# How a head's queries, keys and values are fetched in an attention core: one broadcast transfer on GpSimd's queue, or two of 64 rows on SyncE's

## The chip, the cores and the metric

The kernel runs on one core of a Trainium2 chip. Its time is the device time of one execution in microseconds; a kernel's figure is the median of its runs. The engines of a core work through their own instruction streams and wait for each other by semaphores: TensorE (PE) multiplies, VectorE (DVE), ScalarE (ACT) and GpSimd (POOL) work on tiles, SyncE (SP) issues transfers. Transfers are carried out by 16 DMA engines, whichever engine issues them.

## The reference

A trunk of two layers on 1024 tokens of 1024 features: a retention layer and a chunked attention layer, each behind an RMSNorm and followed by an MLP with squared ReLU, and a last norm. The change is in the attention:

```python
def _chunk_attention(h, w_in, rel_bias, w_out):
    q, k, v = jnp.split(h @ w_in, 3, axis=-1)          # 16 heads of 64 features
    ...
    def one_chunk(c):                                  # 64 queries, the 576 keys up to their chunk's end
        s = jnp.einsum('bqhd,bkhd->bhqk', qb, kb) * scale + bias[None]
        s = jnp.where(valid, s, -jnp.inf)
        p = jax.nn.softmax(s, axis=-1)
        return jnp.einsum('bhqk,bkhd->bqhd', p, vb)
    o = lax.map(one_chunk, jnp.arange(nc))
    return o @ w_out
```

## The kernel before, in words

Everything is float32. Each operand of a product is split into a high part, rounded to the tensor engine's float32r, and a low part, the rest; three products (lines 162 to 164, one each of high-high, low-high and high-low) carry a full one.

The attention has two stages. The **projection** computes queries and keys for pairs of heads (`qk_proj`) and then values. A result `t` is split into `dhi` and the remainder (lines 727 and 729), and SyncE stores both to scratch tensors in DRAM (line 733): `qA` for queries, `kA` for keys, `vA` for values (line 756). A stored key tensor of a head is `[64 features, 2 parts, 1024 tokens]`. Weights come in units of 512 KB (`wraw`, line 146, two buffers), also issued by SyncE, and are split by ACT (`whi`, line 137) and DVE or POOL (`wlo`, line 141).

The **core** goes over 16 heads with four units each; a unit `g` holds two blocks of 128 queries. Each head needs four things, loaded by `load_head`: `qh` (128 x 1024: high and low queries, 64 features each, stacked on the partitions), `kk` (128 x 2 x 1024: the high keys and the low keys, both on the upper and on the lower 64 partitions, so that two passes give all four partial products), the bias `bt`, and the values `vst`. `qh`, `kk` and `bt` have two buffers each, `vst` three: the keys of head h go where those of head h-2 were, and the transfer can start once TensorE has read those for the last time. In a unit, lines 846 and 847 compute scores into `pS`, line 851 (DVE) adds the bias and takes the extreme, line 855 (ACT) the exponentials, line 857 (POOL) scales them; line 875 (PE) transposes them to `pt`, ACT and DVE split the result, and line 887 (PE) multiplies by the values. One step of the output projection of earlier heads (`att_out`, the filler, lines 162 to 164 with `oh`, `ol`) is issued with each unit from the 19th unit on.

The order in which instructions stand on each engine is decided by a scheduler from the order of the code and its own estimate of the times; each engine then works through its list in that order. The queues of SP and POOL are lists of this kind: a transfer that waits for its buffer holds back all that stands behind it on that queue.

Heads 0 and 1 are fetched ahead, during the projection; the others within the core.

Of the kernel before, what the change touches and what calls it, by code (L numbers as in the profile page):

```python
# [9 lines left out]
F32 = mybir.dt.float32  # L10
# [3 lines left out]
PSUM = bass.MemoryType.PSUM  # L14
DRAM = bass.MemoryType.DRAM

P = 128
# [9 lines left out]
DH = 64  # L27
# [15 lines left out]
def _tables():  # L43
    """Position tables: they depend on the shapes alone."""
    import numpy as np

    half = DK // 2
    inv = np.exp(-np.float32(np.log(10000.0)) * np.arange(half, dtype=np.float32) / np.float32(half))
    ang = (np.arange(S, dtype=np.float32)[:, None] * inv.astype(np.float32)[None, :]).astype(np.float64)
    cos = np.cos(ang).T.astype(np.float32)  # L50
    sin = np.sin(ang).T.astype(np.float32)
    lg = _log_gamma()
    jp = np.arange(S) % HT
    vdec = np.exp(-lg[None, :] * (jp[:, None] + 1.0)) * RET_SCALE
    vdec = vdec.reshape(NB, P, RH).transpose(1, 0, 2)
    ip = np.arange(HT)
    odec = np.exp(lg[None, :] * (ip[:, None] + 1.0)).reshape(HT // P, P, RH).transpose(1, 0, 2)
    j = np.arange(P)[:, None]
    i = np.arange(P)[None, :]
    same = (j // CHUNK) == (i // CHUNK)  # L60
    mask = np.zeros((P, RH, P))
    for h in range(RH):
        m = np.where(i >= j, 1.0, 0.0)
        mask[:, h, :] = np.where(same & (i < j), np.exp(2.0 * lg[h] * (j - i)), m)
    f = lambda a: np.ascontiguousarray(a, dtype=np.float32)
    return {
        "cos": f(cos),
        "sin": f(sin),
        "vdec": f(vdec),
        "odec": f(odec),  # L70
        "odec2": f(odec * odec),
        "mask": f(mask),
    }
# [3 lines left out]
def trunk_kernel(ctx: ExitStack, tc: tile.TileContext, I, out):  # L77
# [34 lines left out]
    def load_gains(psp, pl, parts, g0):  # L112
        """Gains of 128 features in a row each, turned so that the features lie on the partitions."""
        n = sum(src.shape[0] for src in parts)
        rows = pl.tile([n, P], F32, name="grows", tag=f"grows{g0}")
        r = 0
        for src in parts:
            DMA.dma_start(out=rows[r:r + src.shape[0], :], in_=src)
            r += src.shape[0]

        def turn():
            pg = psp.tile([P, n], F32, name="pg", tag="ps")
            nc.tensor.transpose(pg, rows, ident[0:n, 0:n])
            nc.vector.tensor_copy(out=gall[:, g0:g0 + n], in_=pg)
        return turn
# [8 lines left out]
    def split(src, hi, lo, hi_eng="act", lo_eng="dve"):  # L134
        """hi: src rounded to the tensor engine's float32r; lo: what is left of src, exactly."""
        if hi_eng == "act":
            nc.scalar.copy(out=hi, in_=src)  # L137
        else:
            nc.vector.tensor_copy(out=hi, in_=src)
        eng = nc.vector if lo_eng == "dve" else nc.gpsimd  # L140
        eng.tensor_tensor(out=lo, in0=src, in1=hi.bitcast(F32), op=ALU.subtract)  # L141

    def wload(src, kb, cols):
        """Fetch one weight unit [128, kb, cols] (1024 columns)."""
        raw = wp.tile([P, kb, cols], F32, name="wraw", tag="wraw", bufs=2)
        DMA.dma_start(out=raw, in_=src.rearrange("(k p) c -> p k c", p=P))
        return raw
# [11 lines left out]
    def mm3(ps, lhs, rhs, start, stop):  # L159
        """Three products that carry a float32 product of split operands."""  # L160
        (lh, ll), (rh, rl) = lhs, rhs
        nc.tensor.matmul(ps, lhsT=lh, rhs=rh, start=start, stop=False)  # L162
        nc.tensor.matmul(ps, lhsT=lh, rhs=rl, start=False, stop=False)  # L163
        nc.tensor.matmul(ps, lhsT=ll, rhs=rh, start=False, stop=stop)  # L164
# [4 lines left out]
    def rsqrt_newton(sd, v, y):  # L169
        """y = v ** -0.5, one Newton step past the square root's table."""  # L170
        nc.scalar.activation(sd, v, AF.Sqrt)
        nc.vector.reciprocal(out=y, in_=sd)
        nc.vector.scalar_tensor_tensor(out=sd, in0=v, scalar=-0.5, in1=y, op0=ALU.mult, op1=ALU.mult)
        nc.vector.tensor_tensor(out=sd, in0=sd, in1=y, op=ALU.mult)
        nc.vector.scalar_tensor_tensor(out=y, in0=sd, scalar=1.5, in1=y, op0=ALU.add, op1=ALU.mult)

# [1 line left out]
    class Norm:  # L178
# [28 lines left out]
        def finish(self, psp, hf, col=False, row=True):  # L207
            """r = rsqrt(mean + eps) of a half: along the free axis in rB, along the partitions in rcol."""
            ah = self.gp.tile([P, HT], F32R, name="ah", tag="ah")
# [18 lines left out]
    def up_group(psp, norm, w, hf):  # L228
        """128 output features of one half of the tokens."""
        hi, lo = w  # L230
        ps = psp.tile([P, HT], F32, name="ps", tag="ps")
        for kb in range(NB):
            mm3(ps, (hi[:, kb, :], lo[:, kb, :]), (norm.hi[kb][hf], norm.lo[kb][hf]), kb == 0, kb == NB - 1)
        return ps
# [5 lines left out]
    def proj_tok(psp, norm, src, evac):  # L240
        """512 output features, tokens on the partitions: one bank for each block of tokens."""
        pss = [psp.tile([P, HT], F32, name="ps", tag="ps") for _ in range(NB)]
# [10 lines left out]
    def down(box, src, nk, rhs, hi_eng="act", lo_eng="dve"):  # L253
        """h += W^T rhs for nk blocks of features, one group at a step. box holds the PSUM pool and, where
        the blocks are final, their norm; blocks that were final before the norm was there follow."""
        cols = 1024 // nk
# [35 lines left out]
    class Filler:  # L292
        """Steps of a product that are issued between other work."""

# [42 lines left out]

    # ================= retention =================
    vS = [dram.tile([S, DV], F32, name=f"vS{i}") for i in range(RH)]
# [137 lines left out]
    with ExitStack() as ph:  # L477
# [6 lines left out]
        with ExitStack() as st:  # L484
# [5 lines left out]

            # Loads run in the order of use, a ring of raw tiles ahead of the splits.
            items = [(hd, hf, what) for hd in range(RH) for hf in range(2) for what in ("q", "k", "v0", "v1")]
# [33 lines left out]
            def turn_k(hd):  # L526
                """Keys of the first half with the tokens on the partitions."""
                kt[hd] = th, tl = [cp.tile([P, 4, DK], F32R, name=n, tag=n, bufs=1) for n in ("kth", "ktl")]
# [45 lines left out]
            def outs(hd, hf, pr):  # L574
                """Retention of two blocks of queries and their normalised rows."""
                pss, mv = [], cp.tile([P, 2, 2], F32, name="mv", tag="mv", bufs=2)
# [115 lines left out]

    # ================= first MLP =================
    with ExitStack() as ph:
# [3 lines left out]

    # ================= chunked attention =================
    w_in = I["att_w_in"][0]  # L700
# [6 lines left out]
    with ExitStack() as ph:  # L707
# [57 lines left out]
        def load_q(hd):  # L765
            T[hd, "q"] = cq.tile([P, S], F32R, name="qh", tag="qh", bufs=2)
            nc.gpsimd.dma_start(out=T[hd, "q"], in_=qA[hd // 2][hd % 2].rearrange("z f c -> (z f) c"))

        def load_k(hd):
            t = cq.tile([P, 2, S], F32R, name="kk", tag="kk", bufs=2)  # L770
            src = kA[hd // 2][hd % 2]
            nc.gpsimd.dma_start(out=t.rearrange("p z s -> p (z s)"), in_=bass.AP(tensor=src.tensor, offset=src.offset, ap=[[0, 2], [2 * S, DH], [1, 2 * S]]))
            T[hd, "k"] = [t[:, 0, :], t[:, 1, :]]
# [18 lines left out]
    with ExitStack() as ph:  # L792
# [7 lines left out]
        with ExitStack() as st:  # L800
# [8 lines left out]
            def load_head(hd, step):  # L809
                """Stacks that give all four partial products of q k in two passes, values and bias."""  # L810
                if step == 0:
# [8 lines left out]
                else:  # L820
                    t = cp.tile([P, NB, P], F32R, name="vst", tag="vst", bufs=3)
                    nc.gpsimd.dma_start(out=t, in_=vA[hd // 8][:, (hd % 8) * P:(hd % 8 + 1) * P].rearrange("(t p) c -> p t c", p=P))
                    T[hd, "v"] = t
# [11 lines left out]
            def scores(hd, g, z):  # L835
                """Probabilities of one block of queries; scores and bias come negated."""
                Q = 2 * g + z
# [97 lines left out]

    # ================= second MLP and the last norm =================
    with ExitStack() as ph:
        psp = pool(ph, "psF", None, 8, PSUM)
        with ExitStack() as st:
# [4 lines left out]
            def last(src, rhs):  # L944
                """The last part of the product, half by half: one half leaves while the other is computed."""
                ws = []
# [63 lines left out]
```

## Time and profile before

| | |
|---|---|
| median of 3 runs | 3041.18 us (3039.38 to 3042.13) |
| span of the profiled execution, first to last instruction | 3039.2 us |
| TensorE busy | 2871.2 us, 94% of the span |
| VectorE, ScalarE, GpSimd busy | 1319.7, 880.3, 432.5 us |
| mean granted clock of TensorE | 0.971 of full speed |
| core stage | about 1900 to 2290 us of the span |
| projection stage | about 1630 to 1900 us |

The span is that of the profiled execution; the time of that execution is not told beside it, and the runs shown lie 0.2 to 2.9 us above the span. A stage in which TensorE is not busy is where time can be won; what ends its idle stretches there is what bounds it.

### The profile page before, as it was taken

The page shows a single profiled execution, that of the slowest core. Times are in us where ns is not written, and L with a number is a line of the kernel's source. Part 1 is how long each engine was busy: PE and PEld are TensorE (multiplying, and loading weights), DVE is VectorE, ACT ScalarE, POOL GpSimd, SP SyncE. Part 2 cuts the span into 40 slices and gives each one's busy share as a digit, 9 for nine tenths or more (in the row PEclk, how much of TensorE's full clock was granted, in tenths as well). Part 3 has the DMA queues.
Part 4 walks back from the last instruction along what each step waited for, and adds up shares of the span by engine and source line. Part 5 has one row for each costly group of instructions (what it writes and reads, how often), then busy time and mean ns, then how long its engine had stood idle before and what let it go on. Part 6 is the DMA issues. An engine that isn't in the chain of part 4 may idle for free.

```text
span 3039.2 us, 33109 instructions
## 1 busy us (share of the span) xinstructions
PE 2871.2 (94%) x13178; PEld 2376.4 (78%) x13178; DVE 1319.7 (43%) x2194; ACT 880.3 (29%) x1484; POOL 432.5 (14%) x439
## 2 busy tenths in 40 slices
PE   8999999899999999999999899576879999999998
PEld 7888888677778888888888788465767888888887
DVE  6331133555565333333346233465668333333335
ACT  4012222432342221112223122564655111222213
POOL 4320000322230000000002000454533000000002
PEclk9999999899999999999999999788989999999999
DMA  4323333432111111111114546645521111111111
GB/s 138 106 87 103 108 105 96 158 104 90 63 49 43 48 49 49 49 49 49 49 46 133 149 147 162 120 95 115 113 68 42 49 49 49 49 46 45 49 49 70
DMA packets 258122, 245.86 MB, mean 81 GB/s; under 512 B 25048, under 2 KB 209440, under 8 KB 255920
## 3 DMA queue, kind: packets, MB, share of 16 engines
q1 hardware_dynamic: 220896, 207.19, 22.4%
q0 software_dynamic: 35584, 33.61, 5.1%
q10 hardware_dynamic: 1488, 2.95, 0.3%
q8 instruction: 103, 1.69, 0.2%
q14 instruction: 51, 0.42, 0.0%
HBM read 189.09 MB, written 57.19 MB: 81 GB/s over the span
## 4 chain that ended last, share of the span: by engine, by line
PE 83%; DMA 10%; DVE 4%; POOL 1%; ACT 1%; issue 1%; SPq 0%; POOLq 0%; ACTq 0%; DVEq 0%
PE ps L162 26%; PE ps L163 26%; PE ps L164 26%; DMA kk<-kA 7%; PE po L887 1%; PE pt L875 1%; DVE hlo L190 0%; DMA kA<-dhi 0%; PE pS L846 0%; POOL acc L200 0%; DMA xt<-in_x_dram 0%; PE pS L847 0%; PE pt L629 0%; DMA wraw<-in_att_w_in_dram 0%; DMA qA<-dhi 0%
## 5 line engine op out<-in xcount | busy, mean ns | idle before, releaser
L162 PE MATMUL ps<-hhi,whi 128*128 128x512 f32 x1792 | 699.3, 390 | 12.5 <-ACT whi L137 9.3
L163 PE MATMUL ps<-hlo,whi 128*128 128x512 f32 x1792 | 698.8, 390 | 1.4 <-DVE hlo L190 1.4
L164 PE MATMUL ps<-hhi,wlo 128*128 128x512 f32 x1792 | 698.5, 390 | 1.0 <-DVE wlo L141 0.9
L137 ACT CAST whi<-wraw 128x1024 fp32r<-128x1024 f32 x220 | 231.6, 1053 | 1255.1 <-PE ps L163 1023.4
L280 DVE TENSOR_TENSOR h<-ps,h 128x512 f32<-128x512 f32 x368 | 253.6, 689 | 467.5 <-PE ps L164 465.4
L162 PEld LDWEIGHTS ps<-hhi,whi 128*128 128x128 f32 x1792 | 337.2, 188 | 83.6 <-ACT whi L137 10.0
L163 PEld LDWEIGHTS ps<-hlo,whi 128*128 128x128 f32 x1792 | 337.3, 188 | 72.1 <-DVE hlo L190 2.1
L164 PEld LDWEIGHTS ps<-hhi,wlo 128*128 128x128 f32 x1792 | 337.1, 188 | 72.2 <-DVE wlo L141 2.1
L162 PE MATMUL ps<-uh,whi 128*128 128x512 f32 x960 | 379.7, 396 | 0.0
L163 PE MATMUL ps<-ul,whi 128*128 128x512 f32 x960 | 379.7, 396 | 0.0
L164 PE MATMUL ps<-uh,wlo 128*128 128x512 f32 x960 | 379.7, 396 | 0.0
L141 DVE TENSOR_TENSOR wlo<-wraw,whi 128x1024 fp32r<-128x1024 f32 x213 | 266.7, 1252 | 239.4 <-ACT whi L137 239.3
L200 POOL TENSOR_TENSOR acc<-acc,sq 128x512 f32<-128x512 f32 x70 | 102.4, 1465 | 1418.0 <-ACT sq L199 1412.2
L324 DVE SCALAR_TENSOR_TENSOR t<-ps,rB 128x512 f32<-128x512 f32 x128 | 88.0, 691 | 320.6 <-PE ps L164 320.6
L162 PEld LDWEIGHTS ps<-uh,whi 128*128 128x128 f32 x960 | 180.3, 188 | 43.7
L164 PEld LDWEIGHTS ps<-uh,wlo 128*128 128x128 f32 x960 | 180.3, 188 | 43.6
L163 PEld LDWEIGHTS ps<-ul,whi 128*128 128x128 f32 x960 | 180.3, 188 | 43.6
L846 PE MATMUL pS<-kk,qh 128*128 128x320 f32 (+1 forms) x192 | 70.0, 370 | 107.2 <-DMA kk<-kA 102.4
L325 ACT ACTIVATE t<-t 128x512 f32<-128x512 f32 x128 | 80.5, 630 | 262.1 <-DVE t L324 262.1
L162 PE MATMUL ps<-whi,hhi 128*128 128x512 f32 x384 | 149.4, 389 | 0.3 <-DVE vt L755 0.3
L164 PE MATMUL ps<-whi,hlo 128*128 128x512 f32 x384 | 149.4, 389 | 0.0
L163 PE MATMUL ps<-wlo,hhi 128*128 128x512 f32 x384 | 149.4, 389 | 0.0
(188 smaller groups left out, 3760.3 us busy)
## 6 DMA issues: line engine op xcount, KB each, us to landing
wraw<-in_mlp_w_dram SPq DMA_DIRECT2D x128, 512.0 KB, 3.7
wraw<-in_ret_w_in_dram SPq DMA_DIRECT2D x48, 512.0 KB, 4.0
kk<-kA POOLq DMA_DIRECT2D x16, 1024.0 KB, 27.4
wraw<-in_att_w_in_dram SPq DMA_DIRECT2D x24, 512.0 KB, 3.9
vS<-t SPq DMA_DIRECT2D x32, 256.0 KB, 2.0
gS<-t SPq DMA_DIRECT2D x32, 256.0 KB, 2.1
wraw<-in_ret_w_out_dram SPq DMA_DIRECT2D x16, 512.0 KB, 3.5
raw<-vS SPq DMA_DIRECT2D x16, 512.0 KB, 4.5
```

The costliest lines, as they stand in the source:

```text
L137: nc.scalar.copy(out=hi, in_=src)
L141: eng.tensor_tensor(out=lo, in0=src, in1=hi.bitcast(F32), op=ALU.subtract)
L162: nc.tensor.matmul(ps, lhsT=lh, rhs=rh, start=start, stop=False)
L163: nc.tensor.matmul(ps, lhsT=lh, rhs=rl, start=False, stop=False)
L164: nc.tensor.matmul(ps, lhsT=ll, rhs=rh, start=False, stop=stop)
L200: nc.gpsimd.tensor_tensor(out=self.acc[hf], in0=self.acc[hf], in1=sq, op=ALU.add)
L280: nc.vector.tensor_tensor(out=hv, in0=ps, in1=hv, op=ALU.add)
L324: nc.vector.scalar_tensor_tensor(out=t, in0=res[hf], scalar=0.0, in1=rB[:, hf * HT:(hf + 1) * HT], op0=ALU.max, op1=ALU.mult)
L325: nc.scalar.activation(t, t, AF.Square)
L846: nc.tensor.matmul(ps[:, y, :hw], lhsT=qs, rhs=kh[:, ks], start=True, stop=False)
L875: nc.tensor.transpose(pt[:, c - done:c - done + P], pr[:, (kb - k0) * P:(kb - k0 + 1) * P], ident)
L887: nc.tensor.matmul(po[:, oc:oc + n], lhsT=T[hd, "v"][:, kb, :], rhs=t[:, off[kb]:off[kb] + n], start=i == 0, stop=i == len(seq) - 1)
```

## The change

The queries and the values of a head are issued by SyncE and no longer by GpSimd. The keys of a head came in one transfer of GpSimd, whose source names the 64 feature rows twice by an outer dimension of two with step 0; now they come in two transfers of SyncE, each of the 64 rows to one half of the partitions. Bytes, buffers and arithmetic are as they were.

```diff
         def load_q(hd):
             T[hd, "q"] = cq.tile([P, S], F32R, name="qh", tag="qh", bufs=2)
-            nc.gpsimd.dma_start(out=T[hd, "q"], in_=qA[hd // 2][hd % 2].rearrange("z f c -> (z f) c"))
+            DMA.dma_start(out=T[hd, "q"].bitcast(F32), in_=qA[hd // 2][hd % 2].rearrange("z f c -> (z f) c"))

         def load_k(hd):
             t = cq.tile([P, 2, S], F32R, name="kk", tag="kk", bufs=2)
             src = kA[hd // 2][hd % 2]
-            nc.gpsimd.dma_start(out=t.rearrange("p z s -> p (z s)"), in_=bass.AP(tensor=src.tensor, offset=src.offset, ap=[[0, 2], [2 * S, DH], [1, 2 * S]]))
+            for z in range(2):
+                DMA.dma_start(out=t[z * DH:(z + 1) * DH].bitcast(F32), in_=src)
             T[hd, "k"] = [t[:, 0, :], t[:, 1, :]]
...
                 else:
                     t = cp.tile([P, NB, P], F32R, name="vst", tag="vst", bufs=3)
-                    nc.gpsimd.dma_start(out=t, in_=vA[hd // 8][:, (hd % 8) * P:(hd % 8 + 1) * P].rearrange("(t p) c -> p t c", p=P))
+                    DMA.dma_start(out=t.bitcast(F32), in_=vA[hd // 8][:, (hd % 8) * P:(hd % 8 + 1) * P].rearrange("(t p) c -> p t c", p=P))
```

`DMA` is `nc.sync`, SyncE's queue. The changed kernel is one line longer, so lines behind 772 count one more there.

On SyncE's queue in the middle of the core there stood only the biases of heads 6 to 9 (`skew_10933` to `skew_10936`) and a unit of the output weights:

```order
L779 DMA bt<-skew_10933 64x576 x2
L779 DMA bt<-skew_10934 64x576 x2
L146 DMA wraw<-in_att_w_out_dram 128x2x512
L779 DMA bt<-skew_10935 64x576 x2
L779 DMA bt<-skew_10936 64x576 x2
```

Now the same place reads, from head 7 on (`kA_10921` holds heads 6 and 7, `kA_10922` heads 8 and 9):

```order
L767 DMA qh<-qA_10913 128x1024
L773 DMA kk<-kA_10921 64x2048 x2
L780 DMA bt<-skew_10934 64x576 x2
L146 DMA wraw<-in_att_w_out_dram 128x2x512
L823 DMA vst<-vA_10909 128x8x128
L767 DMA qh<-qA_10914 128x1024
L773 DMA kk<-kA_10922 64x2048 x2
L780 DMA bt<-skew_10935 64x576 x2
L823 DMA vst<-vA_10909 128x8x128
L767 DMA qh<-qA_10914 128x1024
L773 DMA kk<-kA_10922 64x2048 x2
```

The values, queries and keys of each head stand ahead of its bias, and the output weights stand ahead of the values of head 8. On GpSimd's queue the loads of head 8 stood between the scalings of probabilities (`pr`) of earlier units; these are the rows before:

```order
L141 TENSOR_TENSOR wlo<-wraw,whi 128x1024
L857 TENSOR_SCALAR pr<-pr,sm 128x384
L822 DMA vst<-vA_10909 128x8x128
L857 TENSOR_SCALAR pr<-pr,sm 128x512
L141 TENSOR_TENSOR ol<-osum,oh 64x256
L767 DMA qh<-qA_10914 128x1024
L857 TENSOR_SCALAR pr<-pr,sm 128x640
L772 DMA kk<-kA_10922 128x1x2048
L857 TENSOR_SCALAR pr<-pr,sm 128x640
```

In the changed kernel the same stretch of GpSimd's queue holds the arithmetic alone, in the same sequence. The third place is SyncE's queue in the projection, where the loads of head 1 (`qA_10910`, `kA_10918`) come in between the stores of the keys of heads 6 and 7 (`kA_10921`) and the value weights; this is a piece of the difference:

```order
-L733 DMA kA_10921<-dhi 64x512 x2
-L733 DMA kA_10921<-t 64x512 x2
-L146 DMA wraw<-in_att_w_in_dram 128x2x512 x4
+L733 DMA kA_10921<-dhi 64x512
+L733 DMA kA_10921<-t 64x512
+L733 DMA kA_10921<-dhi 64x512
+L733 DMA kA_10921<-t 64x512
+L146 DMA wraw<-in_att_w_in_dram 128x2x512
+L767 DMA qh<-qA_10910 128x1024
+L773 DMA kk<-kA_10918 64x2048 x2
+L146 DMA wraw<-in_att_w_in_dram 128x2x512 x3
```

Three transfers of 512 KB stand there between the first and the second of four weight units. The loads of head 0 are spread over the same queue a little earlier, among the stores of the key and query tensors of heads 4 to 7. On TensorE, VectorE and ScalarE the sequence is that of before but for the first two dozen or so units of the core, where neighbouring steps change places.

## Rows read from the trace of the kernel before

**Rows 1.** The page: the span, and the chain that ended last by line.
```profile
span 3039.2 us, 33109 instructions
...
PE ps L162 26%; PE ps L163 26%; PE ps L164 26%; DMA kk<-kA 7%; PE po L887 1%; PE pt L875 1%; DVE hlo L190 0%; DMA kA<-dhi 0%; PE pS L846 0%; POOL acc L200 0%; DMA xt<-in_x_dram 0%; PE pS L847 0%; PE pt L629 0%; DMA wraw<-in_att_w_in_dram 0%; DMA qA<-dhi 0%
```
**Rows 2.** Waits, 1880 to 2310 us: total us, times, longest us.
```profile
PE pS L846 <- DMA kk<-kA: 102.4, 8, 15.5
```
**Rows 3.** Timeline of PE: start us, us; in brackets the idle time before.
```profile
1941.32 0.47 PE L846 MATMUL pS<-kk,qh 128*128 128x128 f32 x1 [15.48 <-DMA kk<-kA]
...
2257.45 0.44 PE L846 MATMUL pS<-kk,qh 128*128 128x128 f32 x1 [8.00 <-DMA kk<-kA]
```
**Rows 4.** Timeline of POOL: two issues of keys, heads 6 and 7.
```profile
2002.65 0.86 POOL L772 DMA_DIRECT2D kk<-kA  x1
...
2036.99 0.86 POOL L772 DMA_DIRECT2D kk<-kA  x1
```
**Rows 5.** Tile `kk`, 1900 to 2300 us: issues on POOL (ns, min/median/max), and landing.
```profile
L772 POOL DMA_DIRECT2D kk<-kA x14: 862/863/884, 1914.1 to 2231.7; - x14
...
DMA to landing us min/median/max: 24.4/27.2/30.3
```
**Rows 6.** Windows: us, busy time per engine, PE clock, DMA share, GB/s.
```profile
2047.00:2052.00 5.00, 5.00 (x37) 4.72 (x36) 4.11 (x13) 4.34 (x10) 4.84 (x5) 1.00 0.14 55
...
15.00:20.00 5.00, 5.00 (x26) 4.13 (x25) 4.89 (x7) 4.29 (x8) 1.11 (x1) 1.00 1.07 373
...
1719.00:1721.00 2.00, 2.00 (x10) 1.65 (x9) 0.69 (x1) 0.09 (x1) 0.00 (x0) 1.00 0.88 184
```
**Rows 7.** Windows of heads: us, PE, PEld, DVE, ACT, POOL busy, clock, DMA share, GB/s.
```profile
1941.30:1957.40 16.10, 15.40 (x92) 14.11 (x92) 11.00 (x32) 12.06 (x30) 8.49 (x14) 0.80 0.22 55
1971.90:2002.90 31.00, 28.98 (x192) 25.25 (x192) 25.22 (x75) 25.39 (x64) 19.38 (x32) 0.95 0.51 101
2037.10:2054.40 17.30, 17.10 (x115) 15.23 (x113) 15.18 (x43) 14.62 (x35) 12.22 (x17) 1.00 0.43 113
...
2257.40:2290.00 32.60, 32.26 (x195) 29.06 (x196) 23.76 (x56) 21.25 (x49) 10.46 (x15) 0.93 0.06 18
```
**Rows 8.** Windows: sum over the five two-head stretches between stalls, heads 5 to 14.
```profile
sum 182.05, PE 180.56 PEld 164.48 DVE 143.89 ACT 134.25 POOL 101.58; mean PE 36.11 PEld 32.90 DVE 28.78 ACT 26.85 POOL 20.32
```
**Rows 9.** Waits, 1690 to 1705 us: total us, times, longest us.
```profile
ACT dhi L727 <- DMA kA<-dhi: 8.2, 1, 8.2
PE ps L162 <- ACT whi L137: 8.0, 1, 8.0
...
ACT whi L137 <- DMA wraw<-in_att_w_in_dram: 4.0, 1, 4.0
```
**Rows 10.** DMA issues, 1667 to 1700 us: count, KB each, median us to landing.
```profile
kk<-kA POOLq DMA_DIRECT2D x2, 1024.0 KB, 29.4
...
kA<-dhi SPq DMA_DIRECT2D x4, 128.0 KB, 13.9
```
**Rows 11.** DMA issues, 1705 to 1730 us, the same columns.
```profile
kA<-dhi SPq DMA_DIRECT2D x7, 128.0 KB, 2.3
```
**Rows 12.** Window after the stall in the projection, columns as in rows 6.
```profile
1701.00:1713.00 12.00, 11.44 (x42) 8.91 (x43) 6.24 (x8) 3.27 (x5) 0.00 (x0) 0.82 0.74 199
```
**Rows 13.** DMA issues, 1900 to 2300 us: queries of the core.
```profile
qh<-qA POOLq DMA_DIRECT2D x14, 512.0 KB, 10.8
```
**Rows 14.** DMA issues of the whole span: a small transfer.
```profile
ext<-in_att_rel_bias_dram ACTq DMA_DIRECT2D x1, 20.0 KB, 1.7
```
**Rows 15.** Timelines of POOL and SP at the core's start: values, last weight unit.
```profile
1903.50 1.85 POOL L822 DMA_DIRECT2D vst<-vA  x2
...
1905.95 0.53 SPq L146 DMA_DIRECT2D wraw<-in_att_w_out_dram  x1
```
**Rows 16.** Tiles `qh` and `vst`: issues on POOL, ns min/median/max.
```profile
L767 POOL DMA_DIRECT2D qh<-qA x16: 538/617/759, 1659.4 to 2230.0; - x16
...
L822 POOL DMA_DIRECT2D vst<-vA x16: 897/974/983, 1903.5 to 2227.1; - x16
```

## The prediction

> **What bounds the kernel now.** I read the chain that ended last first. It is TensorE nearly throughout, but 7% of the span in it is one transfer, the keys of a head, `kk<-kA` [rows 1]. The waits say where: in the core TensorE stood idle eight times for keys, 102.4 us in total [rows 2], first for 15.48 and last for 8.00 us, each time at the first score of a head [rows 3]. Next I asked why the keys are late, by their issue or by their transfer. Keys for head 7 are issued at 2036.99 us, when head 5 ends; those of head 6 at 2002.65, when head 4 ends [rows 4, 7]. So GpSimd issues them the moment the buffer is free; it is not late. The transfer itself takes 24.4 to 30.3 us [rows 5], and an undisturbed head takes 17.30 [rows 7]. Thirty less 17.3 is the stall of about 13. It comes only with every second head, since the keys of the next one travel during the stall.
>
> Why is the transfer slow? From 2047 to 2052 one key transfer is the main traffic: 0.14 of 16 engines, 55 GB/s [rows 6]. That is 2.2 engines. Elsewhere in the same trace 373 GB/s pass with all engines at work [rows 6]. The transfer is not short of bandwidth; it sits on two engines, as many as its source has outermost copies. The Trainium skill, "DMA: Bandwidth & Descriptors", section "Rules for kernel authors", says that a leading broadcast dimension of c copies confines a transfer to at most c engines; by that rule the old transfer has two engines and each new one, with 64 rows outermost, sixteen; the trace agrees, with 0.14 of 16.
>
> **What a head costs without the stall.** In head 6, which follows no stall, TensorE is busy 17.10 of 17.30 us at clock 1.00, while VectorE has 15.2, ScalarE 14.6 and GpSimd 12.2 [rows 7]. TensorE bounds there, so 17.30 us is the floor of a head with filler.
>
> **The change, part by part.**
>
> *Keys in two halves on SyncE.* The trace has no 64-row load of this size. The nearest row is the stores of 64 rows to `kA` and `qA`: 184 GB/s at a share of 0.88 [rows 6]. A small transfer lands in 1.7 us [rows 14]. Estimate for 1.05 MB at 184 GB/s: 5.7 us, and 1.7 of latency, 7.4 us; the queries ahead of them, 0.52 MB at 373 GB/s, add 1.4. Some 9 us after the buffer is free, against 17.3 that a head gives. The pessimistic bound is the median of 10.8 us that 512 KB of queries took in the core [rows 13], beside the slow key transfers: two in a row are 21.6 us. I take the store rate, since the reason of the 10.8, the long key transfers, is gone. So the keys land before they are needed: **-102.4 us**.
>
> A rule stands against the split. The Trainium skill, same page and section, advises against two transfers to the halves of the partitions: they serialize on the same engines, and one of 128 partitions is better. By it the halves would give nothing over one full transfer; since the old transfer had two engines and not sixteen, they still gain here, and the sum would be the same unless the old one was already as fast as two halves, which is a rival below. No run here shows the split against one full transfer.
>
> *TensorE's clock.* After each stall it runs at half clock for some us. The five stretches of two heads between stalls took 182.05 us [rows 8] against 10 x 17.30 = 173.0: 9.0 us. The last head with its tail, 32.6 us at 0.93 [rows 7], hides 2.3. Heads 2 to 4, 16.1 us at 0.80 and 31.0 at 0.95, hide 3.2 and 1.6, but there ScalarE and VectorE are nearly as full as TensorE, and I count half, 2.4. Together **-13.7** (9.0 to 16.1).
>
> *The projection.* The two first key transfers, issued about 1667 to 1669, take 29.4 us, and meanwhile stores of 128 KB land in 13.9 us [rows 10]; later ones take 2.3 [rows 11]. ScalarE waited 8.2 us for such a store, then 4.0 for weights queued behind stores on SyncE, and TensorE 8.0 us for ScalarE [rows 9]. Twelve us at 0.82 follow, 2.2 us more [rows 12]. Every store uses engines that the keys hold. With the keys on all engines and issued later this goes: up to -10.2. But now 3 MB of keys and queries stand on SyncE between stores and value weights. A weight unit held behind one of 512 KB waits 1.4 to 2.8 us more (373 and 184 GB/s), which the second buffer covers. I take **-9** (0 to -10.2).
>
> *The start of the core.* The values of head 0 were issued by GpSimd at 1903.50; now they stand behind the last weight unit of SyncE, which goes out at 1905.95 [rows 15]: some 3 us later. And the keys of head 2 have a short lead: issued at 1914.1 [rows 5], needed at 1941.32 - 15.48 = 1925.8 [rows 3], 12 us, beside the values of three heads and a unit of weights. **+3** (0 to +6).
>
> *Queues.* GpSimd loses 48 issues: 16 x (0.617 + 0.863 + 0.974) = 39 us [rows 5, 16]. It has 12.2 of 17.3 us to do in a head and TensorE does not wait for it: 0. If that cover were gone, in heads 0 to 4, it could give some 5 us. SyncE gets 64 issues of the cost of its weight issues, 0.53 us [rows 15], 34 us in a queue that mostly waits. Its new waits are the buffers: a query load waits for TensorE's last score of head h-2. Behind it stand the keys, the bias, the output weights and the next values; all of them are needed at least a head later, so nothing that is due waits. The output weights stand ahead of the values of head 8 and wait for GpSimd's `wlo`, which stands before the scores that free the buffers. 0.
>
> Sum: -102.4 - 13.7 - 9 + 3 = -122.1. From 3039.2: a span of 2917.1. The median of the runs lies 2.0 us above the span; I add that: **2919 us**.
>
> **Rivals.**
>
> *Loads still late.* If queries and both halves take the 21.6 us of the pessimistic bound, a stall of 21.6 - 17.3 = 4.3 us stays with every second head, 8 times: 34 us, and some 8 of slow clock: 2961. For it: 2.3 MB a head in 17.3 us are 133 GB/s without a pause. Against it: 373 GB/s were reached. Smaller remainders lie between.
>
> *The projection does not gain, or loses.* Keys on the stores' own queue delay them and the weights as much as before: the 9 us stay, 2928; or the stall grows by as much again, 2937. For it: that stage has TensorE busy and little slack. Against it: two halves of 2.8 us in place of one transfer of 29.
>
> *The split gives nothing.* If two halves one after the other take as long as the old transfer, 27.2 us [rows 5], the stalls stay: 3041. For it: the bytes are the same. Against it: at a share of 0.14 the old transfer leaves most engines to be gained. The Trainium skill's rule on halves, above, speaks for it only where the one transfer already uses all engines.
>
> *Slower.* If each half of 64 rows runs on one engine, at 55/2 = 27 GB/s, it takes 19 us, and if both use the same engine, a head's keys hold it for 39 us. From 24.4 us on (the mean distance of two key issues, from 1914.1 to 2231.7 over 13 [rows 5]) it is slower than now: 39 - 24.4 = 14.6 us a head, 14 heads, 204 us: 3245. Against it: the stores of 64 rows use 0.88 of all engines [rows 6].
>
> **Chances and range.** Forecast 0.70; loads still late 0.11; the projection 0.14; no gain 0.03; slower 0.02. The forecast's own bounds: -102.4 - 16.1 - 10.2 and 5 less for GpSimd gives 2907; -102.4 - 9.0 - 0 + 6 gives 2936. The upper end takes in part of the late loads: **2907 to 2945**. A measurement of this kernel tells about 0.2% from no change, 6 us. Faster 0.95 (forecast, projection, late loads), same 0.03, slower 0.02.
>
> **What will show it.** Right: no wait of TensorE for `kk` in the core; keys landing within some 10 us at a share of engines far above 0.14; every head from 5 on at 17.3 us with clock 1.00; the core shorter by some 113 us; stores of the projection landing in about 2 to 5 us and no wait of 8 us for `whi`. Wrong: stalls for `kk`, `qh` or `vst` in place of the old ones; heads longer than 17.3 with TensorE busy less; a new wait of TensorE on value weights between 1690 and 1800; SyncE waiting long with due loads behind it.

## The result, and the profile after

The changed kernel takes 2915.09 us (median of 4 runs, 2913.94 to 2916.7) against 3041.2 us for the kernel before in the same runs: a ratio of 0.9585, 95% interval 0.9572 to 0.9599. The profiled execution has a span of 2913.1 us, 126.1 less than before; 2919 was forecast, a span of 2917.1. The median lies 2.0 us above the span.

The page of the changed kernel begins with the span, TensorE's busy time and the chain that ended last by engine and by line:

```profile
span 2913.1 us, 33150 instructions
...
PE 2853.9 (98%) x13178; PEld 2360.5 (81%) x13178; DVE 1318.6 (45%) x2194; ACT 879.7 (30%) x1484; POOL 395.5 (14%) x391
...
PE 89%; DVE 5%; ACT 3%; POOL 1%; DMA 1%; issue 1%; SPq 0%; POOLq 0%; ACTq 0%; DVEq 0%
```

The 7% that the chain gave to `kk<-kA` [rows 1] have gone; TensorE is busy for 98% of the span, where it was 94%. GpSimd has lost 37.0 us of work, the 48 issues. The waits of TensorE from 1880 to 2310 us, the stretch of [rows 2], name no keys any more; of all loads of a head only one of values is left:

```profile
PE pS L847 <- DVE sm L852: 4.8, 4, 3.6
PE pt L876 <- DVE ptl L141: 3.1, 9, 0.8
PE ps L163 <- DVE hlo L190: 1.4, 1, 1.4
PE po L888 <- DMA vst<-vA: 0.9, 1, 0.9
```

The keys' tile shows why. Each half lands 8.1 us after its issue, against 27.2 for the whole before [rows 5]:

```profile
L773 SPq DMA_DIRECT2D kk<-kA x32: 450/510/602, 1701.3 to 2116.0; - x32
...
DMA to landing us min/median/max: 5.8/8.1/11.2
```

Windows of the changed kernel (us, busy time of PE, PEld, DVE, ACT and POOL, granted clock, DMA share, GB/s): the whole core, from its first score to its last product with the values; heads 4 to 14; and 3.4 us in which both halves of a head's keys are on their way, its queries having landed 3.9 us after their issue.

```profile
1892.44:2160.30 267.86, 256.75 (x1728) 231.13 (x1727) 228.76 (x643) 219.80 (x535) 146.76 (x224) 0.99 0.56 144
1947.40:2134.60 187.20, 184.06 (x1242) 167.41 (x1243) 162.48 (x455) 152.87 (x373) 104.87 (x160) 1.00 0.59 153
2050.60:2054.00 3.40, 3.40 (x24) 3.12 (x24) 2.69 (x10) 2.56 (x8) 2.17 (x4) 1.00 0.96 210
```

These queries and keys were issued by SyncE, the queries in 0.34 us (start, duration):

```profile
2047.08 0.34 SPq L767 DMA_DIRECT2D qh<-qA  x1
2047.47 1.09 SPq L773 DMA_DIRECT2D kk<-kA  x2
```

The window over the whole core of the kernel before reads:

```profile
1900.12:2285.20 385.08, 273.93 (x1729) 247.40 (x1727) 230.03 (x643) 220.49 (x535) 180.92 (x268) 0.84 0.47 100
```

Subtract the two. The core is 117.2 us shorter. TensorE's idle time in it was 385.08 - 273.93 = 111.2 us and is 11.1: 100.0 us. Its busy time for the same matmuls fell from 273.93 to 256.75: 17.2 us, as the mean clock went from 0.84 to 0.99. The core also begins 7.7 us earlier, at 1892.44 in place of 1900.12. That leaves 1.2 of the 126.1 us elsewhere.

The 7.7 us come from the projection. From 1655 to 1705 us, which takes in the stretch of [rows 10], stores of a key part now land in 2.4 us, not 13.9 (KB each, median us to landing), and TensorE waits for nothing at all between 1660 and 1890 us, where 8.0 stood [rows 9]:

```profile
kA<-dhi SPq DMA_DIRECT2D x12, 128.0 KB, 2.4
```

The stage itself gained more than 7.7 us. Its first result is split (`dhi`) at 1650.8 us in the kernel before and at 1653.5 in the changed one, as the tile's lines show (before, then after):

```profile
L727 ACT CAST dhi<-t x32: 615/620/627, 1650.8 to 1901.1; 128x512 fp32r<-128x512 f32 x32
...
L727 ACT CAST dhi<-t x32: 614/620/626, 1653.5 to 1893.4; 128x512 fp32r<-128x512 f32 x32
```

From there to the core's first score it is 249.3 us before and 238.9 after, 10.4 less. The 2.7 us lost ahead of it lie in stages that the change does not touch; the same point varies from 1650.8 to 1654.0 over the runs here, apart from one that has fewer temporaries. This length, from the first `dhi` to the first score, is called the length of the projection below.

### The profile page after: what moved, and what is told of

It is laid out like the page before. It is cut to its first block, busy times and chain, and to the rows that moved or that the text cites. A ratio compares the mean times of both kernels' runs of the same rounds, so it can differ in the third digit from the quotient of the medians.

```text
span 2913.1 us, 33150 instructions
## 1 busy us (share of the span) xinstructions
PE 2853.9 (98%) x13178; PEld 2360.5 (81%) x13178; DVE 1318.6 (45%) x2194; ACT 879.7 (30%) x1484; POOL 395.5 (14%) x391
## 4 chain that ended last, share of the span: by engine, by line
PE 89%; DVE 5%; ACT 3%; POOL 1%; DMA 1%; issue 1%; SPq 0%; POOLq 0%; ACTq 0%; DVEq 0%
PE ps L163 28%; PE ps L162 28%; PE ps L164 28%; PE po L888 1%; PE pt L876 1%; ACT pr L856 1%; ACT pth L137 1%; PE pS L847 1%; DVE hlo L190 1%; PE pS L848 1%; DVE pr L852 0%; POOL acc L200 0%; DMA xt<-in_x_dram 0%; DVE ptl L141 0%; PE pt L629 0%
## 5 line engine op out<-in xcount | busy, mean ns | idle before, releaser
L200 POOL TENSOR_TENSOR acc<-acc,sq 128x512 f32<-128x512 f32 x70 | 102.4, 1464 | 1419.7 <-ACT sq L199 1413.9
L141 DVE TENSOR_TENSOR ul<-t,uh 128x512 fp32r<-128x512 f32 x128 | 88.3, 692 | 80.6 <-ACT uh L137 80.6
```

The lines of the kernel that those rows point to most:

```text
L200: nc.gpsimd.tensor_tensor(out=self.acc[hf], in0=self.acc[hf], in1=sq, op=ALU.add)
```

## The experiments

The forecast rests on the **shape** of the key transfer: with 64 rows outermost it uses all DMA engines, and the stalls vanish on whichever queue it stands. The rival is the **queue**: transfers issued by SyncE are quicker or come earlier, and the shape matters less. The first two kernels part these. The others test the terms of the sum, and what sets the old transfer's damage. All ratios are to the kernel before in runs on the same chip: it took 3046.25 us beside `shape_alone`, `queue_alone`, `early_old` and `core_old`, 3040.31 beside `values_only` and `core_old_v`, and 3044.55 beside the other four.

**The shape alone.** The kernel before, with the keys in two halves, everything still on GpSimd's queue:

```diff
-            nc.gpsimd.dma_start(out=t.rearrange("p z s -> p (z s)"), in_=bass.AP(tensor=src.tensor, offset=src.offset, ap=[[0, 2], [2 * S, DH], [1, 2 * S]]))
+            for z in range(2):
+                nc.gpsimd.dma_start(out=t[z * DH:(z + 1) * DH], in_=src)
```

> Keys in two transfers of 64 rows, but everything stays on GpSimd's queue. If the number of DMA engines is the cause (my theory): nearly the whole gain, 2910 to 2925 us, no wait of TensorE for keys, and a key half lands in under 12 us. If moving the issue to SyncE is the cause (rival): the stalls stay, 3030 to 3045 us.

Measured: 2914.54 us (2912.44 to 2917.76), ratio 0.9571 (0.9554 to 0.9588). TensorE waits for no keys in the core. The keys' tile:

```profile
L773 POOL DMA_DIRECT2D kk<-kA x32: 515/577/580, 1670.2 to 2121.6; - x32
...
DMA to landing us min/median/max: 4.9/6.6/11.2
```

The interval takes in the 0.9585 of the whole change. The shape carries all of the gain, moving to the other queue adds nothing to it, and the 41 us that GpSimd is busy beyond the changed kernel, with issues, cost nothing.

**The queue alone.** All loads on SyncE, the keys still in one transfer with the copies outermost:

```diff
-            for z in range(2):
-                DMA.dma_start(out=t[z * DH:(z + 1) * DH].bitcast(F32), in_=src)
+            DMA.dma_start(out=t.rearrange("p z s -> p (z s)").bitcast(F32), in_=bass.AP(tensor=src.tensor, offset=src.offset, ap=[[0, 2], [2 * S, DH], [1, 2 * S]]))
```

> Everything issued by SyncE, but the keys still in one broadcast transfer with an outer dimension of two. My theory: each key transfer still sits on two engines, about 20 us or more at 53 GB/s. If all of them take the same two engines, these carry 0.52 MB of keys and some 0.08 MB of the rest per head, 0.605 MB at 26.5 GB/s = 22.8 us a head, so the core goes at 22 to 24 us a head and TensorE waits for keys at every head: 2980 to 3040 us. Rival, the queue is the cause: 2910 to 2925 us.

Measured: 3082.44 us, ratio 1.0123 (1.0101 to 1.0145): 1.2% slower than before, and outside the 2980 to 3040 us that were expected. There are 14 stalls now, one for each head, and not eight:

```profile
PE pS L846 <- DMA kk<-kA: 130.7, 14, 12.3
```

The issue of the next head's queries, 0.34 us in the changed kernel, holds SyncE for 6 to 8 us here, and the keys stand behind it. In SyncE's timeline (start, duration) and then TensorE's (in brackets the idle time before):

```profile
2038.25 6.03 SPq L767 DMA_DIRECT2D qh<-qA  x1
2044.34 0.54 SPq L772 DMA_DIRECT2D kk<-kA  x1
...
2065.43 8.14 SPq L767 DMA_DIRECT2D qh<-qA  x1
2073.63 0.54 SPq L772 DMA_DIRECT2D kk<-kA  x1
```

```profile
2075.21 0.45 PE L846 MATMUL pS<-kk,qh 128*128 128x128 f32 x1 [7.37 <-DMA kk<-kA]
```

Keys issued at 2044.34 free TensorE at 2075.21, 30.9 us later, and the next ones go out at 2073.63, as these land. So one key transfer follows the other, a head takes about as long as a transfer (29.3 us between these two issues, where 22 to 24 were expected), and each head stalls. On GpSimd two were on their way at once during a stall, which is why only every second head stalled there; a window inside a stall of the kernel before has twice the share and bytes of the 0.14 and 55 GB/s of [rows 6]:

```profile
2062.00:2067.00 5.00, 0.00 (x0) 0.00 (x0) 0.00 (x0) 0.00 (x0) 0.00 (x0) 0.50 0.28 103
```

For what SyncE's issue of 6 to 8 us waits, no row says.

**The two early heads as before.** The changed kernel, but queries and keys of heads 0 and 1, fetched during the projection, in the old shape and on GpSimd:

```diff
...
+            if hd < 2:
+                nc.gpsimd.dma_start(out=t.rearrange("p z s -> p (z s)"), in_=bass.AP(tensor=src.tensor, offset=src.offset, ap=[[0, 2], [2 * S, DH], [1, 2 * S]]))
+            else:
+                for z in range(2):
+                    DMA.dma_start(out=t[z * DH:(z + 1) * DH].bitcast(F32), in_=src)
```

> Queries and keys of heads 0 and 1 as before, on GpSimd with the broadcast, the other heads as in the changed kernel. My theory: the slow stores and the wait for weights in the projection come back, TensorE idle 8 us there and the clock low behind it: 2922 to 2927 us, the core as after. Rival, the gain of 7.7 us up to the core's start came from elsewhere: 2913 to 2917 us.

Measured: 2926.74 us (2924.73 to 2929.66), ratio 0.9611 (0.9594 to 0.9628): as expected, 11.6 us above the changed kernel and 12.2 above `shape_alone`, which was run beside it. The stall of the projection is back, in DMA issues (1665 to 1710 us) and TensorE's timeline:

```profile
kk<-kA POOLq DMA_DIRECT2D x2, 1024.0 KB, 33.2
...
kA<-dhi SPq DMA_DIRECT2D x7, 128.0 KB, 8.0
kA<-t SPq DMA_DIRECT2D x6, 128.0 KB, 14.3
```

```profile
1706.06 0.80 PE L162 MATMUL ps<-hhi,whi 128*128 128x512 f32 x1 [12.20 <-ACT whi L137]
```

The projection is 254.6 us long, 15.7 more than in the changed kernel and 5.3 more than before. So two old transfers, far from any wait for keys, cost some 12 us. `shape_alone` also issues these loads on GpSimd, and its projection has no such wait and is 239.0 us long; so it is the shape here too. That the stores are slow because they share engines with the keys is argued from their landing times and not shown by itself.

**Everything but the early heads as before, and what that left open.** The mirror image: heads 0 and 1 new, queries and keys of heads 2 to 15 old (`core_old`; the values stay on SyncE).

```diff
...
+            if hd >= 2:
+                nc.gpsimd.dma_start(out=t.rearrange("p z s -> p (z s)"), in_=bass.AP(tensor=src.tensor, offset=src.offset, ap=[[0, 2], [2 * S, DH], [1, 2 * S]]))
+            else:
+                for z in range(2):
+                    DMA.dma_start(out=t[z * DH:(z + 1) * DH].bitcast(F32), in_=src)
```

> Queries and keys of heads 0 and 1 as in the changed kernel, those of heads 2 to 15 as before; the values on SyncE. My theory: the stalls of the core come back in full, the projection keeps its 8 to 10 us: 3028 to 3036 us. Rival, part of the core's gain came from the values on SyncE: under 3020 us.

Measured: 3014.72 us (3013.1 to 3020.91), ratio 0.9903 (0.9883 to 0.9923), 13 to 21 us under what was expected and within the rival's forecast, that the values on SyncE have a part in the core's gain. Its waits show seven stalls where the kernel before has eight:

```profile
PE pS L853 <- DMA kk<-kA: 90.4, 7, 17.7
```

GpSimd's timeline in the kernel before, around the issue of the keys of head 3, shows where the eighth came from:

```profile
1927.40 0.62 POOL L767 DMA_DIRECT2D qh<-qA  x1
1928.09 0.79 POOL L857 TENSOR_SCALAR pr<-pr,sm 128x640 f32<-128x640 f32 x1
1943.95 0.73 POOL L141 TENSOR_TENSOR ol<-osum,oh 64x256 fp32r<-64x256 f32 x1 [15.07 <-ACT oh L137]
1944.63 0.88 POOL L772 DMA_DIRECT2D kk<-kA  x1
```

and TensorE's:

```profile
1971.89 0.45 PE L846 MATMUL pS<-kk,qh 128*128 128x128 f32 x1 [14.45 <-DMA kk<-kA]
```

The queries of head 3 go out at 1927.40, but its keys stand behind a split of `ol`, which waits 15.07 us for ScalarE, and that ends only after TensorE's first stall [rows 3]. So these keys are issued some 17 us late, and TensorE waits for them until 1971.89 as well, 14.45 us. To see whether it is the values on GpSimd's list that bring this about, two more kernels: the kernel before with the values alone on SyncE (`values_only`), and `core_old` with the values back on GpSimd (`core_old_v`).

```diff
-                    nc.gpsimd.dma_start(out=t, in_=vA[hd // 8][:, (hd % 8) * P:(hd % 8 + 1) * P].rearrange("(t p) c -> p t c", p=P))
+                    DMA.dma_start(out=t.bitcast(F32), in_=vA[hd // 8][:, (hd % 8) * P:(hd % 8 + 1) * P].rearrange("(t p) c -> p t c", p=P))
```

> The kernel before, with the values alone moved to SyncE; queries and keys as before on GpSimd. If taking the value issues from GpSimd's list lets the keys of head 3 be issued before the stall of head 2 (my theory for the stall that is missing in core_old): seven stalls in place of eight, 3022 to 3030 us. Rival, what saved it there were the early loads of heads 0 and 1: 3036 to 3045 us.

> As core_old, but the values on GpSimd as before, so that the core is wholly that of before and only the loads of heads 0 and 1 are new. By my theory the eighth stall is back: 3028 to 3036 us. By the rival, the early loads: 3012 to 3018 us.

Measured: `values_only` 3027.9 us (3022.68 to 3029.19), ratio 0.9951 (0.9937 to 0.9966), with seven stalls; `core_old_v` 3028.13 us (3025.15 to 3028.77), ratio 0.9952 (0.9936 to 0.9969), with eight. Both came out as expected, `core_old_v` at the edge of its range. The waits of `values_only`, then of `core_old_v`, and GpSimd's timeline of `values_only`:

```profile
PE pS L846 <- DMA kk<-kA: 90.1, 7, 15.4
...
PE pS L853 <- DMA kk<-kA: 99.8, 8, 16.6
```

```profile
1931.07 0.86 POOL L772 DMA_DIRECT2D kk<-kA  x1
1931.98 0.80 POOL L857 TENSOR_SCALAR pr<-pr,sm 128x640 f32<-128x640 f32 x1
1932.87 0.72 POOL L141 TENSOR_TENSOR ol<-osum,oh 64x256 fp32r<-64x256 f32 x1
1946.92 0.37 POOL L857 TENSOR_SCALAR pr<-pr,sm 128x128 f32<-128x128 f32 x1 [13.34 <-DVE sm L856]
```

With the values off GpSimd's queue the keys of head 3 are issued ahead of the long wait, and one stall goes. In `core_old_v`, as before, they follow it, at 1934.82. So one stall of the eight belonged to the order of GpSimd's list, and the seven others to the transfer's duration. The early loads by themselves are worth about 12 us by `core_old_v` too; its projection is 239.1 us long, where that of `values_only` has 249.4.

**One transfer of 128 rows.** Does the split itself cost anything? Here the projection stores the keys twice, and a head's keys come in one transfer with 128 rows outermost:

```diff
...
-            for z in range(2):
-                DMA.dma_start(out=t[z * DH:(z + 1) * DH].bitcast(F32), in_=src)
+            DMA.dma_start(out=t.bitcast(F32), in_=src.rearrange("c f z s -> (c f) z s"))
```

> Keys are stored twice in DRAM (32 pairs of stores more in the projection), so that a head's keys come in one transfer of 128 rows. If one full transfer uses ports that two halves leave idle: it lands in 4 to 6 us where the halves take 8, and the time does not change, since the keys are early anyway: 2912 to 2920 us, or 1 to 8 us more if the added stores hold the projection up. If halves are as good: it lands in 7 us or more.

Measured: 2941.56 us, ratio 0.9665 (0.965 to 0.9679): well above the 2912 to 2928 us expected, while the landing came out as for halves that are as good. DMA issues of 1880 to 2330 us, and TensorE's waits from 1660 us on:

```profile
kk<-kA SPq DMA_DIRECT2D x14, 1024.0 KB, 7.4
```

```profile
PE ps L162 <- ACT whi L137: 15.8, 1, 15.8
PE pt L879 <- POOL pr L861: 7.5, 2, 7.2
```

One transfer of 1024 KB lands in 7.4 us, two of 512 KB in 8.1 each, the second issued half a microsecond behind the first. The Trainium skill, "DMA: Bandwidth & Descriptors", section "Rules for kernel authors", says that two halves serialize on the same engines and one transfer of 128 partitions is to be preferred; the trace agrees in so far as the split gains nothing on a full transfer; it loses some 1.2 us. Of the 26 us more, 20 are in the projection, which stores the keys twice and is 258.9 us long; 15.8 of them are one wait. The core is 6 us longer, with a wait of 7.2 us for GpSimd's `pr` in it. So this run compares the landings; a kernel with one full transfer and the projection as it was is not among the runs.

**The old transfer, a head earlier.** The kernel before with three buffers for keys and each head's keys issued one head sooner (room is made by taking `tmp` from five buffers to two):

```diff
-            t = cq.tile([P, 2, S], F32R, name="kk", tag="kk", bufs=2)
+            t = cq.tile([P, 2, S], F32R, name="kk", tag="kk", bufs=3)
...
+        load_k(2)
...
-                    if (hd, "k") not in T:
-                        load_k(hd)
+                    if hd >= 2 and hd + 1 < AH:
+                        load_k(hd + 1)
```

> The old broadcast transfer on GpSimd, but with three key buffers, each head's keys issued a head earlier (the temporaries of the norms get two buffers in place of five to make room). My theory, a stall is what the transfer takes beyond its lead: the lead is now some 30 us or more against 27, so TensorE waits for keys less than 20 us in total, and the core takes 270 to 295 us; the projection keeps its stall of 8 us: 2925 to 2960 us, more if the fewer temporaries cost outside the core. Rival, the slow transfers also disturb what runs beside them: the core stays over 330 us.

Measured: 2982.19 us, ratio 0.9801 (0.9786 to 0.9815). That is above the 2925 to 2960 us expected. TensorE waits for no keys in the core, though they take longer than before, a median of 30.9 us against 27.2; so a stall is indeed the transfer less its lead. The first line of the waits of 1880 to 2310 us and a line of the DMA issues show what comes in place of it:

```profile
PE pS L847 <- DMA qh<-qA: 23.3, 6, 6.6
```

```profile
qh<-qA POOLq DMA_DIRECT2D x14, 512.0 KB, 19.5
```

The queries now take 19.5 us, against 10.8 [rows 13] and 4.4 in the changed kernel. So the hidden key transfers slow down what passes beside them: the core takes 299.4 us, 31.5 more than in the changed kernel and just over the 270 to 295 expected. The other 34.9 us are ahead of the core, which begins at 1927.30: 6.4 ahead of the projection and 28.5 in it, where TensorE waits 24.3 us for `whi`. The temporaries are not those of the norms alone, as was expected; the projection's results `t` are among them, and VectorE, which writes these, now waits for stores to read the last ones out; before it waited 0.8 us for such a store (waits of 1640 to 1930 us):

```profile
DVE t L725 <- DMA qA<-t: 39.8, 6, 14.0
```

How much of that is the fewer temporaries and how much the third old transfer beside the stores, no run parts.

**Halves that do not divide well.** To see by what a half of 64 rows gets all engines, each half was cut in two parts, of 57 and 7 rows, and of 61 and 3; bytes and queue stay:

```diff
-                DMA.dma_start(out=t[z * DH:(z + 1) * DH].bitcast(F32), in_=src)
+                for r0, r1 in ((0, 57), (57, DH)):
+                    DMA.dma_start(out=t[z * DH + r0:z * DH + r1].bitcast(F32), in_=src[r0:r1])
```

> As the changed kernel, but each half of the keys comes in transfers of 57 and 7 rows. If the number of engines follows from the divisors of the row count, 57 rows use 3: those carry 0.39 MB a head, 14.8 us at 26.5 GB/s, less than the 17.0 of a head with filler and about the 14 of heads 2 to 4: 2913 to 2930 us, with keys landing in 12 to 17 us. If every row count spreads over all engines: 2913 to 2918 us and 8 us.

> As rows57, with transfers of 61 and 3 rows. If the divisors decide, 61 rows use one engine, and both halves the same one: 1.08 MB at 26.5 GB/s, 40.8 us a head; the core of 14 heads is bound by it: 3190 to 3260 us, slower than before the change. If both halves take different engines: some 21 us a head, 2960 to 3000. If every row count spreads: 2913 to 2918.

Measured: with 57 rows 2963.18 us (2952.28 to 2974.38), ratio 0.9735 (0.9703 to 0.9768); with 61 rows 3348.54 us, ratio 1.1001 (1.0983 to 1.102). Both are slower than expected by any of the theories, 2930 and 3260 us at most; with 61 rows 32.6 us of it are one wait in the projection. TensorE's waits in the core with 57 rows, then with 61, and a window inside a stall of the latter:

```profile
PE pS L848 <- DMA qh<-qA: 14.2, 4, 4.3
PE pS L848 <- DMA kk<-kA: 11.5, 5, 4.8
```

```profile
PE pS L848 <- DMA kk<-kA: 301.7, 12, 28.8
```

```profile
2100.00:2116.00 16.00, 0.00 (x0) 0.00 (x0) 0.00 (x0) 0.00 (x0) 0.00 (x0) 0.50 0.08 29
```

In that stall a share of 0.08 of 16 engines, 1.3 engines, moves 29 GB/s, and a head takes some 44 us, where 40.8 were expected. The slower rival's mechanism exists, then: 61 rows go one engine's way. They come without a broadcast, so it is the count of rows outermost that makes a transfer slow, and not that its source names rows twice. Cutting three rows off a half makes a kernel slower than before. With 57 rows, stretches late in a head show a share that is three sixteenths:

```profile
2072.00:2080.00 8.00, 7.78 (x53) 6.70 (x51) 6.89 (x16) 6.01 (x15) 4.25 (x7) 1.00 0.19 69
2092.00:2100.00 8.00, 7.48 (x51) 6.79 (x50) 6.88 (x19) 6.80 (x17) 4.67 (x7) 1.00 0.19 75
```

The Trainium skill, same page, section "Why a DMA increments its semaphore by 16 and not by 1", says that the number of engines is the largest number up to 16 that divides the outermost sizes of both sides; that gives 1 for 61, 3 for 57 and 16 for 64, and the trace agrees, with shares of 0.08, 0.19 and 0.96. So the count of engines for 57 rows was right, and the cost was not: stalls remain, and the heads take 20.6 us in place of the 14.8 reckoned for the three engines.

## Why the prediction was right, and where it was off

**The cause.** Right: the transfer sat on two engines, and the shape is what frees it. `shape_alone` has the whole gain; `queue_alone` loses 1.2%. That all loads may stand on SyncE at no cost was right for the new shape; with the old shape it would have been wrong.

**The stalls, -102.4.** They went whole, with no load taking their place but 0.9 us for values; TensorE's idle time in the core fell by 100.0 us, as idle time of other causes rose by 2.4. The landing was forecast at 7.4 us, 9 with the queries ahead; 8.1 was measured for each half.

**The clock, -13.7.** Under-sized: TensorE's busy time in the core fell by 17.2 us, past the upper bound of 16.1. The term took an undisturbed head at 17.30 us, one head's length. In the changed kernel heads 4 to 14 take 187.20 / 11 = 17.02 us each, so that of the 182.05 us [rows 8] not 9.0 but 182.05 - 170.2 = 11.9 were in excess. So 17.30 us was not the floor of a head that the prediction took it for.

**The projection, -9.** The stage is 10.4 us shorter, a little past the upper bound of 10.2; the core starts only 7.7 earlier, since 2.7 were lost ahead of the stage. The experiment that undoes it costs some 12 in the whole. The mechanism was as told: beside the old key transfers stores land in 8 to 14 us, and in 2.4 without; that shared engines are the reason is the prediction's reading still.

**The start of the core, +3.** Over-sized. The values of head 0 came later than needed, as said, but cost the 0.9 us of the wait shown above; the keys of head 2, for which a short lead was feared, have no wait.

**The sum.** The core was forecast at -102.4 - 13.7 + 3 = -113.1 and measured at -117.2; the projection -9 and -10.4; elsewhere 0, and +2.7 ahead of it and -1.2 behind the core. The span is 4.0 us below the forecast, and the median of 2915.09 lies 3.9 below 2919. That it is no further off is in part luck: the clock and the projection gave 4.9 us more than forecast, and the 2.7 us ahead of the stage, which have nothing to do with the change, hide half of that.

**A sentence that was wrong.** "So GpSimd issues them the moment the buffer is free; it is not late" holds for heads 6 and 7 that were looked at, not for head 3: its keys went out behind 15.07 us of waiting on GpSimd's own list. One of the eight stalls had that cause. It did not show in the total, since a fast transfer and a free queue each remove this stall: `shape_alone` leaves the keys on GpSimd's queue and has no stall either.

**The rivals.** Loads still late, and a projection that does not gain: neither came; keys land in at most 11.2 us, and 17 were to be had. No gain: refuted, with both halves of the keys on their way the share is 0.96. Slower by one engine per half: not with 64 rows, but `rows61` shows the mechanism.

## What to carry to other kernels

When a transfer is late, divide its rate by that of a busy moment in the same trace, and its DMA share by one sixteenth, before looking at who issues it: two engines' share at 55 GB/s, beside 373 elsewhere, called for another outermost dimension, and no queue, buffer or earlier issue was worth as much. A slow transfer that is hidden can still charge what passes beside it, here some 12 us in another stage whose stores came late, and 23.3 us through the next head's queries. And check when a transfer is issued at each of its places, not at two of fourteen: where it shares a list with arithmetic, one long wait in that list can make it late once.

## What the runs showed of the chip, unexpected

- An issue of queries on SyncE, a median of 0.34 us in the changed kernel, takes a median of 7.8 and up to 9.7 us when the key transfers are of the old shape, and 3.6 and up to 8.3 with halves of 57 rows; queries issued by GpSimd beside old key transfers took at most 0.759 us [rows 16]. With transfers of the old shape the kernel is 36 us slower with all loads on SyncE than with all on GpSimd, in runs side by side. Why the issue is held was not settled, nor whether two old transfers on SyncE's queue would share the same two engines.
- With halves of 57 rows the share in the two windows above is that of three engines, and a head needs 20.6 us. The three were reckoned to carry 0.39 MB each; at the 23 to 25 GB/s of one of them in these windows that is an estimated 16 to 17 us. What makes up the rest was not tried.
